# Rotary rotation of key and query tiles handed over 13 steps behind the eviction instead of 7

## The chip, the cores and the metric

The kernel runs on one core of a Trainium2 chip. The metric is the device time of one execution in microseconds (us), smaller is better. The engines are named as in the profile: PE multiplies matrices, PEld is its loading of weights, DVE (VectorE) and ACT (ScalarE) do elementwise work, POOL (GpSimd) does a few small operations, and SP (SyncE) issues the DMAs. Each engine works through its own queue of instructions.

## The reference, cut to what matters

The reference is a trunk of two layers over 256 tokens of width 2048. In each layer one input projection of the normalised `x` feeds two groups of heads: an RWKV-7 scan in both directions, and attention in a window with four key/value heads and sixteen query heads of width 64. Both outputs are gated, joined and sent through one output projection. The part around the change is the rotary position on the attention's keys and queries:

```python
def rope(t, positions):            # half = 32
    ang = positions[:, :, None] * inv
    cos, sin = jnp.cos(ang), jnp.sin(ang)
    t1, t2 = t[..., :half], t[..., half:]
    return concatenate([t1 * cos - t2 * sin, t2 * cos + t1 * sin])
...
    qh = rope(q, positions)
    kh = rope(k_at, positions)
    y_at = window_attention(qh, kh, vh, sink[l])
```

## The kernel before, in words

Everything is kept transposed, 128 channels on the partitions and 256 tokens along the free axis. Products of float32 accuracy are made from parts: a weight tile is split into a high part (ACT, line 221) and a low part (DVE, line 223), the activations likewise, and three matmuls (lines 291 to 293) add up one 128x256 tile. Such three matmuls are one **projection step**; 16 steps make a tile of 128 output channels, and then the tile's eviction function is called.

`Stream` (lines 240 to 273) holds the queue of all projection steps. `run(n)` does n of them. `later(n, fn)` puts `fn` on a timer; the timer is counted down at the end of each step, the one that called `later` included. So `later(7, ...)` calls the function after the sixth step behind the tile's last one, and `later(10, ...)` after the ninth.

The other work of a layer is put between the steps. `window(64, ...)` (line 393) cuts 64 steps into 14 groups of four or five; ahead of each group it advances generators that issue one piece each: `scan_p`, `scan_i` and `scan_b` are three stages of the RWKV scan, `attend` the attention. The order on PE is the order in which the program issues (`manual_schedule`). On the other engines a scheduler chooses the order while the program is built, by its own model of when each instruction will be ready; the chip then runs each engine's list strictly in that order. Instructions issued through `PA` and `PV` (class `InTurn`, line 236) keep the program's order among themselves; in the profile all of them carry line 236 and are told apart by their tiles.

A layer's input tiles come in this order: two low-rank tiles, 32 tiles for the scan in eight windows, the value weights in the first half of a ninth window, the key tiles k0 and k1 in its second half, the query tiles q0 to q3 in a tenth window, and then g0, q4, g1, q5, g2, q6, g3, q7, g4 to g7, gates and queries in turn, in three more. So k0, k1, q0, q1, q2, q3 follow each other every 16 steps, and q4 to q7 come every 32.

The eviction of a key or query tile is `rope_evac` (line 523). It copies the tile from PSUM to `raw` (tile `u`, two buffers, ACT, line 532). Four DMAs on SP's queue (line 534) copy its quarters of 32 partitions, pairwise exchanged, to `rot` (tile `rrot`, one buffer). `turn` (lines 537 to 540) is three DVE instructions: `raw` times the cosines, `rot` times the sines, and their sum in `raw`. `parts` (lines 542 to 544) splits the result into a high part (ACT, into `kr`, or `KA` for keys) and a low part (DVE, into `iu`, `du`, `iuh`, `duh`, or `kd`, `kkr` for keys), which the attention's scores (line 1034) read. `turn` and `parts` are issued by the timers.

The scan's chain on PE that appears below: `scan_i` turns between products in PSUM (`pq`, `pd`, `pf`), which wait for copies by DVE into `tv` (line 907) and by ACT into `QF` and `tt` (lines 900, 868); `scan_b` makes a product `pcc` that waits for ACT's `suv` (line 972). Weight tiles arrive by DMAs on the same SP queue (line 213, `raw<-wi`), into three buffers.

Of the kernel before, what the change touches and what calls it, by code (L numbers as in the profile page):

```python
# [133 lines left out]
def hybrid_trunk_kernel(ctx, tc, xT, wi, wv, wo, par, fing, dup, iup, sink, pos, cst, out):  # L134
# [24 lines left out]
    def st(tag, shape, dt=F32, bufs=1):  # L159
        return sp.tile([128, *shape], dt, tag=tag, name=tag, bufs=bufs)  # L160
# [114 lines left out]
    S = Stream()  # L275
# [145 lines left out]
    def queue_inputs(l):  # L421
# [101 lines left out]
        def rope_evac(place):  # L523
            def evac(pm):
                if not rope:
                    rope.extend((st("TW", [T]), st("XA", [T])))
                    V.tensor_tensor(rope[0], COS, L.norm.rb, op=ALU.mult)
                    V.tensor_tensor(rope[1], SIN, L.norm.rb, op=ALU.mult)
                CR, SR = rope
                raw = st("u", [T], bufs=2)  # L530
                rot = st("rrot", [T])
                A.activation(raw, pm, AF.Copy)
                for q in range(4):
                    SY.dma_start(out=rot[q * 32 : q * 32 + 32, :], in_=raw[(q ^ 1) * 32 : (q ^ 1) * 32 + 32, :])  # L534
                hi, lo = place()

                def turn():
                    PV.tensor_tensor(raw, raw, CR, op=ALU.mult)
                    PV.tensor_tensor(rot, rot, SR, op=ALU.mult)
                    PV.tensor_tensor(raw, raw, rot, op=ALU.add)  # L540

                def parts():
                    PA.activation(hi, raw, AF.Copy)
                    PV.tensor_tensor(lo, raw, hi.bitcast(F32), op=ALU.subtract)

                S.later(7, turn)
                S.later(10, parts)

            return evac

# [692 lines left out]
```

## Time and profile before

| what | value |
|---|---|
| median of 3 runs | 1202.62 us (1201.23 to 1203.34) |
| the profiled execution | 1201.32 us, of which span 1199.5 us |
| mean granted clock of PE | 0.991 |
| rotation DMAs (`rrot<-u`) | 80 of 32.0 KB, 2.1 us to landing (median) |
| `hi` splits on ACT, `lo` splits on DVE | 560 each, 624 and 686 ns (mean) |

The span runs from the first to the last instruction. A timeline row gives the start, the duration, the engine, the line, the operation, its tiles as out<-in, and in brackets the idle time of that engine just before it with what ended it. In rows that merge several DMA issues the duration covers all of them. A row of the waits gives the engine that waited, at which tile, for whom, the total, how often, and the longest.

### The profile page before, as it was taken

The numbers are of one execution on the slowest core, as the hardware profiler recorded it, in microseconds if no ns is written. First come the engines' busy times: TensorE is split into PE (matmuls) and PEld (weight loads), VectorE is DVE, ScalarE is ACT, GpSimd is POOL, SyncE is SP. The second block draws the span as 40 slices with busy tenths as digits, with TensorE's granted clock in tenths as the row PEclk, the third lists the DMA queues.
The fourth block names the chain that finished last, engine by engine and source line by source line (L and its number), as shares of the span: only waits on it lengthen the run. The fifth ranks groups of instructions, "written<-read, shape, count | busy, mean of one in ns | idle before, by whom it ended". The sixth has DMA issues, their size and how long they took to land. (4 is left out here: it accounts for less than half of the span.)

```text
span 1199.5 us, 38085 instructions
## 1 busy us (share of the span) xinstructions
PE 1165.4 (97%) x16151; PEld 1087.2 (91%) x16151; DVE 910.2 (76%) x2019; ACT 776.3 (65%) x1953; POOL 18.9 (2%) x23
## 2 busy tenths in 40 slices
PE   8999999999999999999999999999999999999996
PEld 6998999999888889999999989999998888889996
DVE  6888888888876668866667978887887766786554
ACT  6666776777776557655555766876777665665553
POOL 0000000000000000000000000000000000000000
PEclk8999999999999999999999999999999999999998
DMA  7553333323333434467655443334323333345653
GB/s 254 163 174 124 107 100 114 118 85 115 110 105 106 129 98 137 143 221 249 214 183 166 133 129 113 100 106 127 115 92 99 116 115 131 113 148 186 212 186 121
DMA packets 60410, 166.63 MB, mean 139 GB/s; under 512 B 7728, under 2 KB 22736, under 8 KB 60240
## 3 DMA queue, kind: packets, MB, share of 16 engines
q1 hardware_dynamic: 60240, 164.21, 42.5%
q8 instruction: 126, 2.06, 0.7%
q14 instruction: 44, 0.36, 0.1%
HBM read 157.37 MB, written 4.19 MB: 135 GB/s over the span
## 5 line engine op out<-in xcount | busy, mean ns | idle before, releaser
L291 PE MATMUL pm<-XH,hi 128*128 128x256 f32 x1664 | 495.9, 298 | 3.4 <-ACT XH L183 1.7
L293 PE MATMUL pm<-XH,lo 128*128 128x256 f32 x1664 | 469.9, 282 | 6.2 <-DVE lo L223 6.2
L292 PE MATMUL pm<-XL,hi 128*128 128x256 f32 x1664 | 469.4, 282 | 0.3
L221 ACT ACTIVATE hi<-raw 128x512 fp32r<-128x512 f32 x560 | 327.7, 624 | 194.9 <-PE pm L292 110.3
L223 DVE TENSOR_TENSOR lo<-raw,hi 128x512 fp32r<-128x512 f32 x560 | 369.7, 686 | 97.5 <-ACT hi L221 91.3
L291 PEld LDWEIGHTS pm<-XH,hi 128*128 128x128 f32 x1664 | 315.0, 189 | 18.5 <-ACT XH L183 2.4
L293 PEld LDWEIGHTS pm<-XH,lo 128*128 128x128 f32 x1664 | 315.4, 190 | 8.8 <-DVE lo L223 8.5
L292 PEld LDWEIGHTS pm<-XL,hi 128*128 128x128 f32 x1664 | 315.4, 190 | 1.1 <-DVE XL L184 1.1
L291 PE MATMUL pm<-MH,hi 128*128 128x256 f32 x512 | 144.1, 281 | 0.0
L293 PE MATMUL pm<-MH,lo 128*128 128x256 f32 x512 | 144.0, 281 | 0.0
L292 PE MATMUL pm<-ML,hi 128*128 128x256 f32 x512 | 143.8, 281 | 0.0
L291 PEld LDWEIGHTS pm<-MH,hi 128*128 128x128 f32 x512 | 96.6, 189 | 0.8 <-issue 0.8
L293 PEld LDWEIGHTS pm<-MH,lo 128*128 128x128 f32 x512 | 96.6, 189 | 0.2 <-DVE lo L223 0.2
L292 PEld LDWEIGHTS pm<-ML,hi 128*128 128x128 f32 x512 | 96.6, 189 | 0.0
L907 DVE CAST_PREDICATED tv<-LV,pd 128x256 f16<-128x256 uint8 x80 | 34.4, 430 | 12.8 <-PE pd L906 12.2
L790 DVE TENSOR_TENSOR ge<-pg,C 128x1024 f32<-128x1024 f32 x32 | 38.9, 1221 | 4.4 <-PE pg L784 4.4
L972 ACT ACTIVATE suv<-pcc 64x128 f32<-64x128 f32 x128 | 34.2, 267 | 11.4 <-PE pcc L970 7.1
L900 ACT ACTIVATE QF<-pq 128x256 f16<-128x256 f32 x80 | 30.8, 384 | 14.3 <-PE pq L864 13.8
L1062 ACT ACTIVATE mv<-mv,mx 128x257 f32<-128x257 f32 x64 | 31.8, 501 | 11.3 <-DVE mx L1059 11.3
L956 ACT ACTIVATE rh<-pcc 128x128 f32<-128x128 f32 x64 | 17.5, 273 | 33.2 <-PE pcc L954 32.8
L784 PE MATMUL pg<-mv,bk 64*128 64x128 f32 x512 | 37.2, 285 | 0.3 <-DVE ge L790 0.3
L784 PEld LDWEIGHTS pg<-mv,bk 64*128 64x128 f32 x512 | 31.1, 187 | 2.4 <-DVE ge L790 0.4
(247 smaller groups left out, 1860.1 us busy)
## 6 DMA issues: line engine op xcount, KB each, us to landing
raw<-wi SPq DMA_DIRECT2D x207, 512.0 KB, 3.8
raw<-wo SPq DMA_DIRECT2D x64, 512.0 KB, 4.2
raw<-wv SPq DMA_DIRECT2D x8, 512.0 KB, 3.7
rrot<-u SPq DMA_DIRECT2D x80, 32.0 KB, 2.1
vg<-xT SPq DMA_DIRECT2D x16, 128.0 KB, 4.2
xd<-vg SPq DMA_DIRECT2D x16, 128.0 KB, 3.5
vg<-xd SPq DMA_DIRECT2D x16, 128.0 KB, 3.7
g<-dup SPq DMA_DIRECT2D x16, 97.0 KB
```

What stands on the lines that cost most here:

```text
L221: A.activation(hi[:, q], raw[:, q], AF.Copy)
L223: V.tensor_tensor(lo[:, q], raw[:, q], hi[:, q].bitcast(F32), op=ALU.subtract)
L291: PE.matmul(pm, wh, rh[:, kk, :], start=(kk == 0), stop=False)
L292: PE.matmul(pm, wh, rl[:, kk, :], start=False, stop=False)
L293: PE.matmul(pm, wl, rh[:, kk, :], start=False, stop=(kk == 15))
L784: PE.matmul(pg[:, h, c * 128 : (c + 1) * 128], BK[half[h], d, c, 1 - h : 3 - h, :].rearrange("p s j -> p (s j)"), MV[half[h], d, c].rearra ...
L790: V.tensor_tensor(GEd(d), pg.rearrange("p h (c x) -> p h c x", c=NC), gm[d].unsqueeze(1).unsqueeze(1).to_broadcast([128, 2, NC, 128]), op= ...
L900: A.activation(t_sub(QF), flat4(pq[:, :, 0:128]), AF.Copy)
L907: V.copy_predicated(t_sub(TC), t_mask, flat4(pd[:, :, 0:128]))
L956: A.activation(RH, pc[:, 0], AF.Copy)
L972: A.activation(here(h), pc[half[h], 1], AF.Copy)
L1062: A.activation(Sc[:, h, q, 0:257], Sc[:, h, q, 0:257], AF.Exp, scale=0.125, bias=mx[:, q : q + 1], accum_out=den[:, q : q + 1])
```

## The change

The two timers are longer. `turn` is issued after the twelfth step behind the tile's last one instead of the sixth, `parts` after the fourteenth instead of the ninth. The eviction, the DMAs, the instructions and their buffers are the same.

```diff
-                S.later(7, turn)
-                S.later(10, parts)
+                S.later(13, turn)
+                S.later(15, parts)
```

## The prediction

> **What bounds the kernel now.** I read the page's first part, then the waits of the whole span, then PE's waits in the stretches where key and query tiles are made, and last the timeline there.
>
> ```profile
> PE 1165.4 (97%) x16151; PEld 1087.2 (91%) x16151; DVE 910.2 (76%) x2019; ACT 776.3 (65%) x1953; POOL 18.9 (2%) x23
> ```
>
> PE is busy in 97% of the span; DVE and ACT have room. So a change that adds and removes no instruction can only move PE's idle time, some 34 us by this line, or its clock. DVE's and ACT's waits count where they make PE wait.
>
> ```profile
> DVE u L236 <- DMA rrot<-u: 17.9, 10, 3.2
> ...
> ACT kr L236 <- DVE u L236: 12.7, 10, 3.0
> ```
>
> The rotation is waited for. DVE stands 17.9 us, in 10 waits, at its first instruction until the exchanged copy has landed, and ACT stands 12.7 us at the high part until DVE is done. Each engine takes its queue in order, so all that stands behind these instructions waits too. Now PE, in the stretch from k0 to q3 of layer 0 (352 to 413 us), just behind it (413 to 490), and from k0 to q3 of layer 1 (938 to 998):
>
> ```profile
> PE pf L864 <- DVE tv L907: 1.7, 2, 1.5
> PE pd L906 <- ACT tt L868: 1.0, 1, 1.0
> PE pq L897 <- DVE tv L907: 0.8, 1, 0.8
> ```
>
> ```profile
> PE pcc L977 <- ACT suv L972: 1.8, 1, 1.8
> PE pm L293 <- DVE lo L223: 1.0, 1, 1.0
> ```
>
> ```profile
> PE pf L864 <- DVE tv L907: 1.2, 2, 1.0
> PE pcc L977 <- ACT suv L972: 0.9, 1, 0.9
> PE pd L906 <- ACT tt L868: 0.8, 1, 0.8
> PE pq L897 <- DVE tv L907: 0.8, 1, 0.8
> ```
>
> None of these rows names the rotation, but `tv`, `tt` and `suv` are what stands behind it. The largest, q3 of layer 0, shows it:
>
> ```profile
> 404.58 2.42 SPq L534 DMA_DIRECT2D rrot<-u  x4
> ...
> 409.80 0.42 DVE L236 TENSOR_TENSOR u<-u,TW 128x256 f32<-128x256 f32 x1 [2.31 <-DMA rrot<-u]
> ...
> 410.59 0.28 PE L293 MATMUL pm<-XH,lo 128*128 128x256 f32 x1
> 410.59 0.43 DVE L236 TENSOR_TENSOR u<-u,rrot 128x256 f32<-128x256 f32 x1
> ...
> 411.05 0.42 ACT L236 ACTIVATE kr<-u 128x256 fp32r<-128x256 f32 x1 [2.96 <-DVE u L236]
> ...
> 412.41 0.54 ACT L972 ACTIVATE suv<-pcc 64x128 f32<-64x128 f32 x2
> ...
> 413.01 0.45 PE L977 MATMUL pcc<-suv,bt 128*64 128x64 f32 x8 [1.78 <-ACT suv L972]
> ```
>
> From the first issue to the landing of the last DMA are 409.80 - 404.58 = 5.2 us. DVE idles 2.31 us of it, ACT 2.96 us at `kr`; `suv`, behind `kr` and two weight splits on ACT, starts at 412.41, and PE has idled 1.78 us. That wait has a second price, in the clock (the number after the engines' busy times):
>
> ```profile
> 413.00:418.00 5.00, 4.99 (x47) 4.64 (x49) 3.34 (x9) 2.15 (x5) 0.00 (x0) 0.66 0.34 105
> 998.00:1003.00 5.00, 5.00 (x57) 4.53 (x53) 4.14 (x13) 1.96 (x5) 0.00 (x0) 1.00 0.41 125
> ```
>
> After the wait of 1.78 us PE has a clock of 0.66 for five us, which loses 0.34 x 5 = 1.7 us of work. Behind the same place of layer 1, where the wait was 0.9, it is 1.00.
>
> **The change, part by part.** *The wait for the DMAs goes.* The four DMAs are issued by the eviction and keep their place in SP's queue; only DVE's three and ACT's one and DVE's one instruction behind them move. Is the copy there when the rotation is now handed over, after the twelfth step? For q3 that step is the matmul row at 410.59, which ends at 410.87, 1.07 us after the landing at 409.80. The tightest of the eight tiles with a real wait is k0 of layer 0:
>
> ```profile
> 358.87 0.43 DVE L236 TENSOR_TENSOR u<-u,TW 128x256 f32<-128x256 f32 x1 [1.25 <-DMA rrot<-u]
> ...
> 359.19 0.28 PE L293 MATMUL pm<-XH,lo 128*128 128x256 f32 x1
> ...
> 359.55 0.28 PE L293 MATMUL pm<-XH,lo 128*128 128x256 f32 x1
> ...
> 362.50 0.51 SPq L534 DMA_DIRECT2D rrot<-u  x1
> ```
>
> Its copy has landed by 358.87, and its twelfth step ends at 359.19 + 0.28 = 359.47, 0.6 us later. So I take DVE's waits for `rrot` as gone. The PE waits listed above are then unsupported, but for the one at `pm` (1.0 us), whose cause is the low split of weights: 1.7 + 1.0 + 0.8 + 1.8 = 5.3 us in layer 0 and 1.2 + 0.9 + 0.8 + 0.8 = 3.7 in layer 1, together **9.0 us**. What is late next in each case is PE itself: `tv` and `tt` have only their own product to wait for, and that was done before the group of steps now stalled behind.
>
> *The clock's dip goes* with the 1.78 us wait: **1.7 us**. [...]
>
> *The moved instructions cost their time elsewhere.* The rotation takes 410.59 + 0.43 - 409.80 = 1.22 us of DVE, the high part 0.42 of ACT, the low part about as much of DVE, as before. By the page DVE has 24% of the span idle, so six rotations a stretch find room. New is the shorter way from `turn` to `parts`: two steps instead of three. A step takes 359.55 - 359.19 = 0.36 us, two take 0.72, the rotation 1.22. ACT then waits at least 0.5 us at the high part, on the 12 tiles from k0 to q3: 6.0 us. Behind ACT's high part are queued the weights' high splits, the next eviction and `suv`; PE waits for those. Today 12.7 us of such ACT waits go with 9.0 us on PE, a share of 0.7, so the upper bound is 6.0 x 0.7 = 4.3. The lower bound is zero, by q4, whose rotation found its copy there:
>
> ```profile
> 433.63 0.42 ACT L236 ACTIVATE kr<-u 128x256 fp32r<-128x256 f32 x1 [0.47 <-DVE u L236]
> ```
>
> ACT waits 0.47 us there, and PE's waits from 413 to 490 us hold none that follows from it. That is the nearest row but in an easier stretch, without `scan_i`; I take **2.0 us**, about the middle. A cost below zero is possible as well: with DVE earlier, the 1.0 us at `pm` in 413 to 490 may shrink; I take nothing for it, and keep 1.0 for the low end.
>
> Edits with one answer: the readers of the high and low parts come tens of steps later (k0 and q0 are first read by the scores a window or two later), so five more steps make no one wait; q7 is the closest with 22 steps between its parts and its scores. POOL's queue holds nothing that moves. `PA` and `PV` instructions of the scan issued in the six steps passed now stand ahead of the rotation, where they no longer wait for its DMA.
>
> **Sum.** 9.0 + 1.7 - 2.0 = 8.7 us. The profiled execution took 1201.32 us, and would take 1192.6. The median of the runs, 1202.62, lies 1.3 above it; the same difference from there gives **1193.9**, which I forecast as the median.
>
> **The rivals.** *A, a part of it:* ACT's new wait bites at its upper bound, since DVE starts the rotation late and ACT is only two steps behind, and the clock dips as before. The gain is 9.0 - 4.3 = 4.7, the time 1197.9. For it: every tile from k0 to q3 has splits of weights behind the high part. Against: at the new places the group's urgent copies were issued at the group's start, ahead of the moved instructions.
>
> *B, nothing:* where DVE does the rotation is the scheduler's choice when it thinks the copy has landed, so a later hand-over leaves the order as it is. Time 1202.6. For it: the row of q5 below shows a rotation done long after its hand-over. Against: in the waiting tiles it stands ahead of its copy's landing by up to 2.31 us in the rows above, so the order there is not one that waits for the landing, and a rotation handed over after 359.47 can't be started at 358.87.
>
> *C, slower:* `rrot` has one buffer. The next tile's DMAs can't be issued until the rotation has read it, SP takes its queue in order, and the weight loads queue behind. k1's first such DMA goes out at 362.50, 3.03 us after k0's twelfth step; less the 1.22 us of the rotation, DVE may begin it 1.8 us after the hand-over without harm. How late can DVE be? q5's rotation was handed over at the end of the row at 448.88:
>
> ```profile
> 448.88 0.28 PE L293 MATMUL pm<-XH,lo 128*128 128x256 f32 x1
> ...
> 453.21 0.42 DVE L236 TENSOR_TENSOR u<-u,TW 128x256 f32<-128x256 f32 x1
> ```
>
> It began 453.21 - 449.16 = 4.05 us later. Were that so in all ten close successions (k0 to k1, and on to q3, in two layers), SP would stand 2.2 us in each, 22 us in all. If all of it reached PE the time would be 1202.6 - 10.7 + 22 = 1213.9; the rival decides from the point where more than half of SP's time reaches PE (10.7 of 22). Against it: the rows of k0 and q3 show DVE idle before the rotation, not late, and the late one belongs to the attention's stretch, where successions are 32 steps long. [...]
>
> **How the numbers follow.** The forecast has 0.67, A 0.16, B 0.10, C 0.07. About 0.2%, 2.4 us, is what a measurement of this kernel can tell from no change. The forecast and A are faster by more, less 0.01 for A's tail: 0.82. No change takes B and that tail: 0.11. Slower is C: 0.07. The low end is the full 9.0 + 1.7 and the 1.0 at `pm`, 1202.6 - 11.7 = 1190.9, taken as 1190.5 for the spread of runs. The high end takes in A and stops short of B at 1201.0, which leaves out B and C, 0.17.
>
> **What would show it.** Right: no wait of DVE at `u` for `rrot` in k0 to q3; the PE waits at `pf`, `pd`, `pq` and `pcc` in the two stretches gone or under 0.3 us each; a clock of 1.00 behind q3; ACT's total wait for DVE `u` near 6 us instead of 12.7. Wrong: DVE's queue in the old order with the same waits (B); ACT's waits for `u` at 12 us or more with PE waits at `tt` and `suv` (A); SP waiting at line 534 for DVE `u`, then PE or ACT for `raw<-wi` (C).

## The result, and the profile after

| | before | after |
|---|---|---|
| median | 1201.95 us (1201.23 to 1203.34, 4 runs) | 1190.43 us (1188.86 to 1191.98, 4 runs) |
| the profiled execution | 1201.32 us, span 1199.5 | 1191.98 us, span 1190.2 |

The ratio after to before is 0.9903, 95% interval 0.9886 to 0.992: the change makes the kernel faster by 11.5 us (9.6 to 13.7 by the interval). The forecast was 1193.9 us; the measured time lies 0.07 us below the low end of its range, 1190.5. In a later comparison on another chip the changed kernel took 1189.74 us beside 1200.11, 10.4 us less, ratio 0.991 (0.9892 to 0.9927); one disturbed execution of 2138 us, the profiled one, is left out there, so that its trace says nothing of the waits.

The first part of the page of the changed kernel, and the rotation's two rows among its waits:

```profile
PE 1163.5 (98%) x16151; PEld 1084.7 (91%) x16151; DVE 909.5 (76%) x2019; ACT 776.9 (65%) x1953; POOL 18.6 (2%) x23
```

```profile
DVE u L236 <- DMA rrot<-u: 4.7, 5, 2.1
ACT kr L236 <- DVE u L236: 4.0, 7, 0.8
```

The engines' work is what it was; DVE's wait for the copy fell from 17.9 us to 4.7 and ACT's behind it from 12.7 to 4.0. PE's waits of the changed kernel from k0 to q3 of layer 0 (350 to 411 us), and then behind that (411 to 486):

```profile
PE pn L928 <- ACT tt L868: 0.2, 1, 0.2
```

```profile
PE pm L293 <- DVE lo L223: 1.0, 1, 1.0
```

From k0 to q3 of layer 1 the row at `pn` is the only one, with the same 0.2. All the rows at `pf`, `pd`, `pq` and `pcc` are gone. New is 0.2 us at `pn` in each layer; the 1.0 at `pm` stays. The five us behind q3 of layer 0 in the changed kernel, with the clock behind the five busy times:

```profile
410.00:415.00 5.00, 5.00 (x63) 4.35 (x62) 4.37 (x17) 2.83 (x9) 0.00 (x0) 1.00 0.68 204
```

PE is busy throughout and the clock is 1.00, where it was 0.66 before.

How the gain comes about is seen best at k0 of layer 0. The kernel before, in the timeline, behind the wait of 1.25 us that the prediction shows:

```profile
361.87 0.42 DVE L907 CAST_PREDICATED tv<-LV,pd 128x256 f16<-128x256 uint8 x1
...
362.35 0.30 PE L864 MATMUL pf<-EYE,tv 64*64 64x32 f16 x16 [1.47 <-DVE tv L907]
```

The changed kernel, the same place:

```profile
359.38 1.28 DVE L223 TENSOR_TENSOR lo<-raw,hi 128x512 fp32r<-128x512 f32 x2
360.58 0.42 DVE L907 CAST_PREDICATED tv<-LV,pd 128x256 f16<-128x256 uint8 x1
...
361.05 0.30 PE L864 MATMUL pf<-EYE,tv 64*64 64x32 f16 x16
...
361.24 0.42 DVE L236 TENSOR_TENSOR u<-u,TW 128x256 f32<-128x256 f32 x1
```

DVE's list now has two low splits and `tv` ahead of the rotation. `tv` starts as soon as DVE has done the splits, PE goes on without a gap, and the rotation, now last, finds its copy there. The order of PE's instructions is the same in both kernels.

### The profile page after: what moved, and what is told of

Read it like the earlier page. It is cut to its first block, busy times and chain, and to the rows that moved or that the text cites. A ratio compares the mean times of both kernels' runs of the same rounds, so it can differ in the third digit from the quotient of the medians.

```text
span 1190.2 us, 38093 instructions
## 1 busy us (share of the span) xinstructions
PE 1163.5 (98%) x16151; PEld 1084.7 (91%) x16151; DVE 909.5 (76%) x2019; ACT 776.9 (65%) x1953; POOL 18.6 (2%) x23
## 4 chain that ended last, share of the span: by engine, by line
PE 68%; issue 15%; DVE 11%; ACT 3%; DMA 2%; POOL 1%; SPq 0%; DVEq 0%; POOLq 0%; ACTq 0%
PE pm L291 17%; PE pm L293 14%; PE pm L292 14%; DVE lo L223 3%; PE pg L784 3%; DMA raw<-wi 2%; DVE kd L236 1%; PE pcc L954 1%; PE py L961 1%; PE py L984 1%; PE pcc L977 1%; PE pcc L967 1%; PE pq L897 1%; DVE lw L236 1%; PE pd L906 1%
```

## The experiments

The theory of the prediction: a wait of DVE for the copy at the old place holds up `tv` (on DVE) and, through ACT's high part, `tt` and `suv`; PE pays for those. Its rivals were a new wait of ACT (A), no change of order (B) and SP held by the single `rrot` (C). Two questions came up with the result: whether the size of the term for ACT's shorter way was wrong, and whether the clock's dip really belongs to the wait. All ratios are against the kernel before, timed on the same chip in the same comparison.

**One tile alone, and all but that one.** e1 gives the new timers to q3 alone, e2 to all but q3; each is this edit with the two pairs swapped:

```diff
-        def rope_evac(place):
+        def rope_evac(place, when=(7, 10)):
...
-                S.later(7, turn)
-                S.later(10, parts)
+                S.later(when[0], turn)
+                S.later(when[1], parts)
...
-                inproj(QG0 + 2 * j, rope_evac(q_place(j)))
+                inproj(QG0 + 2 * j, rope_evac(q_place(j), (13, 15) if j == 3 else (7, 10)))
```

> Only q3 is handed over late (13 and 15), the nine other tiles as before (7 and 10). Theory W, that each tile's gain is its own wait for the exchanged copy plus what that wait does to the clock: PE's waits at pcc for suv go (1.8 us in layer 0, 0.9 in layer 1) and the half-speed stretch of 3.4 us behind q3 in layer 0 with them (1.7), 4.4 us together, about 1197.5; the other PE waits at pf, pd and pq stay at 6.3 us. Rival O, that the gain comes from the order of the other instructions as a whole and not from single waits: no such split, anything from 0 to the full 11 us. Rival K, that the clock's dip does not hang on this wait: 2.7 us, about 1199.2, with the dip still in the trace.

> The other half: all tiles late but q3, which stays at 7 and 10. Theory W: PE's waits at pf, pd and pq go (3.5 us in layer 0, 2.8 in layer 1, 6.3 together), those at pcc (1.8 and 0.9) and the dip of the clock stay; about 1195.7. The two halves add up to the whole change. Rival O: no adding up. Rival K: the dip goes here, or stays away by chance, whatever q3's wait is.

e1 took 1196.03 us, ratio 0.9963 (0.995 to 0.9976): 5.0 us below the 1201.01 of the kernel before on that chip. e2 took 1192.66, ratio 0.9933 (0.9918 to 0.9948): 8.35 below. Both gained more than theory W gave them (1197.5 and 1195.7). Together they gain 13.3 us, more than the 11.5 of the whole change; by their intervals, 2.9 to 6.0 and 6.2 to 9.8, the runs cannot tell whether the halves add up exactly. PE's waits of e2 from k0 to q3, layer 0 and then layer 1:

```profile
PE pcc L977 <- ACT suv L972: 1.5, 1, 1.5
```

```profile
PE pcc L977 <- ACT suv L972: 0.7, 1, 0.7
```

The stalls at `pcc` belong to q3 and the others to the other tiles: q3's two waits at `pcc` are all that is left in e2 (beside the 0.2 at `pn`), and they are what is gone in e1. Nothing is handed on to a later tile. The dip behind q3 is gone in e1 together with its wait (clock 1.00 in 410 to 420 us, 0.83 in the kernel before). But the clock does not simply follow a wait: e2, which should have kept the dip, has a wait of 1.5 us at `pcc` and no dip behind it (1.00 in 410 to 420 us), and e1 has a wait of 2.0 us at `pf` in 361 to 364 us, longer than the 1.78 of the kernel before, and no dip there either:

```profile
360.00:370.00 10.00, 7.97 (x160) 7.28 (x161) 7.12 (x15) 4.33 (x10) 0.00 (x0) 1.00 0.42 137
```

**Other delays.** e3 has 9 and 12 steps (two of the six steps by which the change moves the rotation), e4 has 13 and 16 (the old distance of three steps between rotation and high part).

```diff
-                S.later(7, turn)
-                S.later(10, parts)
+                S.later(9, turn)
+                S.later(12, parts)
```

> A smaller delay: the rotation after 8 steps, the parts after 11. Theory W: two steps are 0.7 us where nothing stands between the steps and up to 2 us where scan products do, so DVE's waits for the copy (18 us in all) fall to about half, and half or more of the 9 us on PE goes: 1193 to 1198. Rival O: the time follows the order that comes out and not the delay, so it may lie anywhere, also above the kernel before.

> The changed kernel with the parts one step later (16), so that three steps lie again between rotation and parts. The prediction's term of 2.0 us for the shorter way says that up to 2 us come back: about 1188.5 to 1190.5, with ACT's wait for DVE u shorter by about 0.4 us on each of the 12 close tiles. If that term was zero in truth, as the changed kernel's trace suggests (PE waits of 0.4 us in all), the time is that of the changed kernel within a microsecond, 1190.4.

e3 took 1197.5 us, ratio 0.9973 (0.9963 to 0.9984); e4 took 1189.75, ratio 0.9909 (0.9893 to 0.9926). e4 against 0.9903 and 0.991 of the changed kernel: one more step between rotation and high part buys nothing that can be measured. But it didn't shorten ACT's wait at the high part as expected (4.7 us, against 4.0 in the changed kernel), so e4 alone doesn't price that wait. e3 brings a surprise. Its wait for the copy, over the span:

```profile
DVE u L236 <- DMA rrot<-u: 21.3, 12, 3.5
```

That is more than the 17.9 of the kernel before, where half was expected, and yet e3 is faster. PE's waits at `pf`, `pd`, `pq` and `pcc` are 5.4 us in its two stretches instead of 9.0, and the mean clock of the span is 0.995, 0.991 in the kernel before. What DVE waits in total isn't what PE pays.

**Later still, one buffer and two.** e5 has 15 and 17 steps; e6 the same, with the copies written to `rrot` and to a free tile in turn.

```diff
+        turns = []
...
-                rot = st("rrot", [T])
+                turns.append(pm)
+                rot = st(("rrot", "acc")[len(turns) % 2], [T])
...
-                S.later(7, turn)
-                S.later(10, parts)
+                S.later(15, turn)
+                S.later(17, parts)
```

> Rotation after 14 steps and parts after 16, which puts the parts behind the next tile's eviction; rrot keeps its one buffer. Rival C, that the one buffer holds SP up: SP's waits for DVE u grow from 8.7 us in the changed kernel by about 0.7 us (two steps) in each of ten successions, to 14 us or more, and the weight loads behind them come late, so the time rises by 2 to 7 us over the changed kernel. Theory W, that only the wait for the copy counted: the wait is gone already at 13, nothing more is won, and SP's standing is covered by the weights that are loaded ahead; within 1.5 us of the changed kernel.

> The same delays, but the copies alternate between rrot and another free tile, so that the next tile's DMAs never wait for the rotation. Rival C: what the one buffer cost comes back, 2 to 7 us against the run with one buffer, and SP's waits for DVE u are gone. Theory W: SP's waits are gone as well but the time is that of the run with one buffer within 1.5 us.

> The changed kernel once more, unaltered, beside the three below. It sets the mark for them: 1189 to 1191.5 us. Theory W says that its trace has, as the first one had, no PE wait over 0.3 us between k0 and q3 and no dip of the clock there.

The three ran on one chip. e5 took 1188.65 us, ratio 0.9902 (0.9887 to 0.9917); e6 1188.3, ratio 0.9899 (0.9884 to 0.9914); the changed kernel 1189.74, ratio 0.991 (0.9892 to 0.9927). The intervals overlap, so e6 is the lowest time measured, but not shown to be faster than the change itself. In e5 and e6 DVE no longer waits for the copy at all, ACT's waits at the high part are 0.4 us, and PE has no wait from k0 to q3. So the 4.7 and 4.0 us of such waits in the changed kernel cost it little: the times are 1.1 and 1.4 us apart, within the intervals. SP's waits at the rotation's DMAs, in the changed kernel and then in e5:

```profile
SPq L534 <- ACT hi L221: 52.3, 18, 7.6
SPq L534 <- DVE u L236: 8.7, 8, 1.3
```

```profile
SPq L534 <- ACT hi L221: 35.0, 12, 8.0
SPq L534 <- DVE u L236: 15.2, 10, 3.4
SPq L534 <- ACT kr L236: 7.1, 6, 2.0
```

Rival C's mechanism is there: SP now stands at line 534 until the rotation has read `rrot`, 8.7 us in all, and in e5 15.2. With two buffers the row for `DVE u` is gone and the time is the same within the intervals. SP would have stood at this line anyway: all its waits there add up to 63.1 us in the kernel before, 61.9 in the changed one, 58.2 in e5 and 58.5 in e6. C has a wait but no price.

**A shorter copy.** e7 keeps 7 and 10 steps and lets POOL issue two of the four DMAs.

```diff
-                    SY.dma_start(out=rot[q * 32 : q * 32 + 32, :], in_=raw[(q ^ 1) * 32 : (q ^ 1) * 32 + 32, :])
+                    (SY, G)[q % 2].dma_start(out=rot[q * 32 : q * 32 + 32, :], in_=raw[(q ^ 1) * 32 : (q ^ 1) * 32 + 32, :])
```

> Delays as before the change (7 and 10), but two of the four DMAs of each tile are issued by POOL instead of SP, so that the copy may land earlier: two issues of 0.6 us each less on SP, 1.2 us earlier if POOL is as quick. Theory W, that the wait and not the place in DVE's list made PE wait: DVE's wait for the copy falls from 18 us to about 8, PE's waits between k0 and q3 from 9 us to 3 or 4, the time to 1195 to 1197. Rival O, that the place in the list is what counts: DVE waits less but PE gains under 2 us. If DMAs from POOL land later than those from SP, the wait grows and the time rises; by theory W it then rises by more than half of what DVE waits longer.

It took 1193.7 us, ratio 0.9938 (0.9916 to 0.996). Its wait of DVE, and PE's waits from k0 to q3 of layer 0:

```profile
DVE u L236 <- DMA rrot<-u: 23.7, 11, 4.1
```

```profile
PE pcc L977 <- ACT suv L972: 0.6, 1, 0.6
PE pf L864 <- DVE tv L907: 0.4, 1, 0.4
```

DVE waits longer than in any other run, where theory W expected 8 us; yet PE's stalls fall from 5.3 us to 1.0 in layer 0 and from 3.7 to 2.7 in layer 1, and the mean clock of the span is 0.995. With other DMAs the scheduler made another list on DVE. So this run is no test of the landing alone; it shows again that the sum of DVE's waits decides nothing without what is queued behind each.

**No wait at the old place.** e8 has the old timers and the four DMAs with their places and sizes, but nothing that has to be waited for. It leaves out the exchanged half's product with the sines, so the keys and queries are not rotated.

```diff
-                rot = st("rrot", [T])
+                rot = st("rrot", [T]); cop = st("acc", [T])
...
-                    SY.dma_start(out=rot[q * 32 : q * 32 + 32, :], in_=raw[(q ^ 1) * 32 : (q ^ 1) * 32 + 32, :])
+                    SY.dma_start(out=cop[q * 32 : q * 32 + 32, :], in_=COS[(q ^ 1) * 32 : (q ^ 1) * 32 + 32, :])
...
-                    PV.tensor_tensor(rot, rot, SR, op=ALU.mult)
+                    PV.tensor_tensor(rot, CR, SR, op=ALU.mult)
```

> The old hand-over (7 and 10 steps), but nothing left to wait for: the four DMAs keep their place, size and count, but copy 32 partitions of the cosine table into a free tile, and the rotation's second product takes CR instead of the exchanged copy. Left out: the exchanged half's product with the sines, so the keys and queries are not rotated. Theory P (a wait at DVE's or ACT's queue costs PE by what stands behind it): all waits of DVE at u for rrot are gone, ACT's at kr fall from 12.7 us to about 5, the stalls at pf, pd, pq and pcc fall under 0.3 us each, and the time is 1189 to 1192 us. Rival Q (the place itself costs, since the rotation's 1.2 us of DVE and 0.4 us of ACT stand ahead of the urgent copies at that place whether they wait or not): half or more of the 9 us at pf, pd, pq and pcc stays, and the time is 1195 to 1199 us.

e8 took 1189.92 us, ratio 0.9913 (0.9896 to 0.993), as the changed kernel. From k0 to q3 of layer 0 it has one row:

```profile
PE pf L864 <- DVE tv L907: 0.3, 1, 0.3
```

Layer 1 has the same one row, with 0.3. The scheduler made DVE's list anew here too: the rotation stands at its old place in k1 and q1, and one to three instructions earlier in the other tiles. So its 1.2 us stand ahead of the urgent copies at least as much as before, and PE doesn't pay for them: the wait is the cause, and rival Q is out. One thing more is different in e8: its DMAs don't wait for the eviction either. Moving the rotation behind the landing (the change) and taking away what it waits for (e8) are worth the same.

**A test of the landing that failed.** e9 is the changed kernel with e7's edit.

> The changed kernel (13 and 15 steps) with two of the four DMAs of each tile issued by POOL. DVE's and ACT's order from k0 to q3 is that of the changed kernel; only the landing of the copy differs. Theory P (place decides): DVE's total wait at u for rrot may change from 4.7 us in either direction, up to 10 us, but the stalls at pf, pd, pq and pcc stay under 0.3 us each and the time lies within 1.5 us of the changed kernel, 1188.5 to 1191.5. Rival L (the landing decides): what DVE waits more for the copy, PE waits too in a share of about a half, so with 4 us or more of added waits the stalls are back with 2 us or more and the time is 1192 or over.

It took 1190.48 us, ratio 0.9919 (0.9903 to 0.9935), with the stalls of the changed kernel; but DVE's waits fell to 2.4 us, so nothing was tested. e10 and e11 were made for that, with four copies more, to a free tile, ahead of the four that are needed:

```diff
-                rot = st("rrot", [T])
+                rot, ahead = st("rrot", [T]), st("acc", [T])
...
-                for q in range(4):
-                    SY.dma_start(out=rot[q * 32 : q * 32 + 32, :], in_=raw[(q ^ 1) * 32 : (q ^ 1) * 32 + 32, :])
+                for to, q in [(ahead, q) for q in range(4)] + [(rot, q) for q in range(4)]:
+                    SY.dma_start(out=to[q * 32 : q * 32 + 32, :], in_=raw[(q ^ 1) * 32 : (q ^ 1) * 32 + 32, :])
```

> The changed kernel (13 and 15 steps) with four more copies of the raw tile, into a free tile, issued ahead of the four that are needed: by SP's 0.6 us for each issue the needed copy lands about 2.4 us later. From k0 to q2 DVE's order is that of the changed kernel. Theory P (place decides): DVE's total wait at u for rrot grows from 4.7 us to 12 or more, and the stalls of PE at pf, pd, pq and pcc from k0 to q3 stay at or under 0.5 us each; the time is 1189 to 1192.5 us. Rival L (length decides): PE waits for about half of what DVE waits, as before the change (17.9 us against 9.0), 4 us or more in the two stretches, and the time is 1194 or over.

> The old hand-over (7 and 10 steps) with the same four copies more, so that the needed copy lands about 2.4 us later, and the scheduler, which reckons with them, now puts the rotation behind one to three more instructions on DVE from k0 to q3 (behind the product of the tile's tv in q1 to q3, but not in k0). Theory P: what decides is the place in DVE's list; with the rotation placed later the stalls at pd and pq go, those at pf may stay, and the time is 1190 to 1198 us, faster than the kernel before though the copy lands later. Rival L: a copy that lands 2.4 us later under the old hand-over makes all waits longer, the stalls grow to 15 us or more, and the time is 1205 or over.

e10 took 1200.07 us, ratio 1.0 (0.9988 to 1.0013): the whole gain is gone. The copy came 2.1 to 4.2 us later than in the kernel before (counted from the start of the eviction, at q0, q1 and q3 of both layers). PE's waits from k0 to q3 of layer 0:

```profile
PE pn L928 <- ACT tt L868: 1.7, 1, 1.7
PE py L984 <- ACT suv L972: 1.3, 1, 1.3
PE pg L784 <- DVE ge L790: 0.3, 1, 0.3
```

With layer 1 (1.5 at `py`, 1.3 at `pn`) they are 6.1 us, over the 4 that rival L named, and the wait of 1.7 us is followed by a dip of the clock (0.60 in 408 to 412 us). The stalls at `pf`, `pd`, `pq` and `pcc` did stay away, as theory P said; but its time did not come true, and the place alone doesn't decide: the trace has ACT's list from k0 to q3 and DVE's from q0 to q2 in the order of the changed kernel, and with the longer waits PE stalls at two other products there. The timeline of e10 at q1 of layer 0 shows the way:

```profile
393.56 0.43 DVE L236 TENSOR_TENSOR u<-u,TW 128x256 f32<-128x256 f32 x1 [3.18 <-DMA rrot<-u]
...
395.30 0.42 ACT L236 ACTIVATE kr<-u 128x256 fp32r<-128x256 f32 x1 [2.81 <-DVE u L236]
...
397.02 0.55 ACT L972 ACTIVATE suv<-pcc 64x128 f32<-64x128 f32 x2
...
397.33 0.74 PE L984 MATMUL py<-suv,ge 128*64 128x64 f32 x8 [1.29 <-ACT suv L972]
```

DVE waits 3.18 us, ACT 2.81 at its high part, `suv` is queued behind that, and PE idles 1.29 us. But the length of the wait isn't the price. By the same trace ACT waits 1.99 us at q2 and PE 1.70, while at q0 and q3 ACT waits 2.20 and 2.75 and no wait of PE of 0.15 us or more follows. Each place has a slack, the time until what is queued behind it is needed, and PE pays for what exceeds that. Compare the changed kernel at q3 of layer 0:

```profile
406.77 0.54 ACT L972 ACTIVATE suv<-pcc 64x128 f32<-64x128 f32 x2
406.93 0.42 DVE L236 TENSOR_TENSOR u<-u,TW 128x256 f32<-128x256 f32 x1 [2.07 <-DMA rrot<-u]
...
407.46 0.28 PE L293 MATMUL pm<-XH,lo 128*128 128x256 f32 x1
...
408.03 0.45 PE L977 MATMUL pcc<-suv,bt 128*64 128x64 f32 x8
...
408.18 0.42 ACT L236 ACTIVATE kr<-u 128x256 fp32r<-128x256 f32 x1 [0.43 <-DVE u L236]
```

DVE waits 2.07 us, as long as at q0 of the kernel before (2.04), which cost PE a microsecond; but `suv` now stands ahead of `kr` on ACT, and PE doesn't wait. e11 took 1209.28 us, ratio 1.0081 (1.0064 to 1.0098), against theory P's 1190 to 1198 too. PE's waits of e11 from k0 to q3 of layer 0:

```profile
PE pd L906 <- ACT tt L868: 2.5, 1, 2.5
PE pf L864 <- DVE tv L907: 1.4, 1, 1.4
```

The scheduler did put the rotation later, about as far as the copy: DVE's total wait, 19.4 us, is near the 17.9 of the kernel before, but ACT's at `kr` grew from 12.7 to 21.8. PE's waits from k0 to q3, 5.3 us in layer 0 and 4.3 in layer 1, are under rival L's 15, though its time held; the mean clock of its span is 0.991, against 0.994 in the changed kernel. Both runs also load SP with four more issues for each tile, and ACT's wait for weights of the input projection is 12.4 us in e10 and 12.3 in e11, against 7.8 in the changed kernel and 10.2 in the kernel before; how much of e10's and e11's time is due to that was not separated. So e10 and e11 show that long waits cost at the new place too, and not how many microseconds belong to the rotation alone.

**The kernel before, twice more.** Its profiled execution was taken again, for the clock.

> The kernel before, unaltered, for a second profiled execution. Theory D (the clock's dip follows the wait of 1.78 us behind q3 in layer 0): the wait is there again with 1.6 to 1.9 us, and behind it the clock stands at half for about 3.4 us again, between 411 and 420 us. Rival K (the dip needs this wait and a chance of where it falls in time): the same wait, but no half clock behind it, or one in another place.

> The kernel before, unaltered, for a third profiled execution, as in the run ahead of it. Theory D: half clock for about 3.4 us behind the wait at q3 in layer 0. Rival K: in some executions only, or in another place.

They took 1202.2 and 1200.57 us. PE's waits in layer 0 (352 to 418 us) of the second execution:

```profile
PE pf L864 <- DVE tv L907: 2.1, 2, 1.9
PE pcc L977 <- ACT suv L972: 1.9, 1, 1.9
PE pd L906 <- ACT tt L868: 0.9, 1, 0.9
PE pq L897 <- DVE tv L907: 0.9, 1, 0.9
```

Of the third, the same stretch:

```profile
PE pf L864 <- DVE tv L907: 2.0, 2, 1.8
PE pcc L977 <- ACT suv L972: 1.5, 1, 1.5
PE pd L906 <- ACT tt L868: 1.0, 1, 1.0
PE pq L897 <- DVE tv L907: 1.0, 1, 1.0
PE pcc L954 <- DVE suv L979: 0.3, 1, 0.3
```

In layer 1 (938 to 1003 us) the rows are the same without the last one, and add up to 4.6 us in the second execution and 3.5 in the third.

The clock behind `pf` and behind `pcc` in layer 0, second execution and then third:

```profile
363.00:367.00 4.00, 4.00 (x28) 3.73 (x28) 2.12 (x4) 0.85 (x2) 0.00 (x0) 0.57 0.60 197
414.00:418.00 4.00, 3.63 (x28) 3.52 (x29) 2.00 (x6) 1.17 (x4) 0.00 (x0) 0.57 0.43 128
```

```profile
363.00:367.00 4.00, 4.00 (x70) 3.73 (x59) 2.66 (x5) 0.87 (x2) 0.00 (x0) 0.65 0.72 185
414.00:418.00 4.00, 3.06 (x41) 2.79 (x41) 3.14 (x8) 2.45 (x7) 0.00 (x0) 1.00 0.26 79
```

The stalls are the same in kind in each execution and vary in size. The second execution has two dips, the third one, and that behind `pf`. Theory D in its simple form, a dip behind q3 each time, is out. Rival K is not shown by these three: the longest single waits (1.78 us in the first; 1.87 and 1.9 in the second; 1.8 in the third) had a dip behind them; q3's 1.5 in the third had none (clock 1.00 in 410 to 420 us), nor had the 1.47 at `pf` in the first (1.00 in 360 to 370). That more than the length of the wait decides is shown by other runs, such as e1 with its 2.0 us and no dip.

## Why the prediction was right in its mechanism, and which steps of its sum failed

*The wait goes.* Right for PE: of the 9.0 us listed at `pf`, `pd`, `pq` and `pcc` all are gone, e1 and e2 show that q3's belong to q3 alone, and e8 that they go with the wait. It was too strong for DVE: "So I take DVE's waits for `rrot` as gone" left 4.7 us, 2.07 of it at q3. The working behind it took the twelfth step for the earliest time of a rotation. It isn't: at q3 DVE stands at the rotation from 406.93 - 2.07 = 404.86 us and starts it at 406.93, while the step's last matmul ends at 407.46 + 0.28 = 407.74. A hand-over gives a place in the program from which the scheduler makes its lists; on the chip only the list holds. The same slip weakened the argument against B, which was right in its outcome.

*The shorter way to the high part.* This is the term of the mechanism that failed: 2.0 us were taken, and the changed kernel shows 0.4, the two rows of 0.2 at `pn`. ACT's waits came out at 4.0 us over the span and 3.1 from k0 to q3, about half of the 6.0 reckoned there. Wrong, too, was the share of 0.7 with which they were carried to PE. That share was measured at the old places. At the new ones `suv` stands ahead of the high part at q3; at q1 and q2 `suv` and `tt` still stand behind it, but waits of up to 0.8 us are within the slack there, as against those of e10. e4 buys nothing with one more step, and e5 and e6, with ACT's waits at 0.4, are 1.1 and 1.4 us faster than the changed kernel, with intervals that overlap. The sum with the measured term is 9.0 + 1.7 - 0.4 = 10.3.

*From one execution to the median.* The profiled execution was forecast at 1192.6 and took 1191.98 us, only 0.6 less, though the term above was 1.6 too large. That is luck: PE lost 0.6 us at a late weight tile at the start of layer 1 (649 us) and 0.6 us more than before ahead of 345 us (9.4 us of idle time there before, 10.0 after), which the prediction didn't reckon with. The larger part of the miss is the last step of the sum, "the same difference from there": the median was put 1.3 us above the profiled execution, and it lies 1191.98 - 1190.43 = 1.55 below it. The runs of one kernel differ by 3 us (1188.86 to 1191.98 here), and the difference between one of them and the median did not carry over to another kernel.

Why the medians differ by 11.5 us, and not by 10.3, stays open. The interval, 9.6 to 13.7 us, holds both, and the later comparison gave 10.4. It may be that the execution that was profiled before the change was a mild one. Its stalls and dip made 9.0 + 1.7 = 10.7 us; the second execution has 5.8 + 4.6 and two dips at 1.7, 13.8; the third 5.8 + 3.5 and one dip, 11.0. But their times, 1201.32, 1202.2 and 1200.57 us, don't follow these sums closely, so it is not shown. The low end of the range, 9.0 + 1.7 + 1.0, was built on the first execution alone, with 1.0 at `pm` that didn't move (it is 1.0 after, too), and so fell short by 0.07 us.

*The clock.* The 1.7 us were right for the profiled execution, but the dip doesn't follow q3's wait each time. In the first trace the clock is 0.50 from 413.73 to 417.14 us, 3.41 us long, and 1.00 from there to 1188.56; in the changed kernel it is 1.00 from 15.15 to 1179.09 us. Behind five single waits of PE a dip lost 1.7 us: behind the 1.78 us of the first execution, the 1.87 and 1.9 of the second and the 1.8 of the third (0.83 over ten us each time), and behind the 1.70 of e10 (0.98 over 403 to 408 us and 0.60 over 408 to 412). Behind e1's 2.0 us it was 1.00 (360 to 370 us), and e7, which has a wait of 1.9 us at `pf` in layer 1, has a mean clock of 0.995 over the span. So the length of a wait doesn't decide alone. Where a wait falls may count too: the changes of the clock in the first trace (4.13, 7.55, 14.37, 413.73, 417.14 and 1188.56 us) lie 1, 2, 117, 1 and 226 times 3.413 us apart, those in the trace of the changed kernel (4.91, 11.74, 15.15 and 1179.09) 2, 1 and 341 times. That the place decides was not shown.

*The rivals.* A lost by its time (1190.43 against 1197.9), but its mechanism is real: with the copy later, in e10, ACT's high part holds `suv` and PE pays. B was out, since DVE's list changed at k0. C's wait of SP came, 8.7 us, with no price. Of the signs named, the clock of 1.00 behind q3 and the waits of PE under 0.3 us came true; DVE without a wait at q3 did not; ACT's total was 4.0 instead of "near 6".

What stays open: the size of the slack at each place, how much of e10's loss is SP's load, why the medians differ by more than the sum, and what beside the length of a wait of PE decides over a dip of the clock.

## What to carry to other kernels

When an instruction that waits for a DMA stands in an in-order queue, look at what is queued behind it and when that is needed, not at the length of the wait: 21.3 us of waiting cost less here than 17.9 had. Hand such work over late enough that its data is there, and test the margin by making the transfer later, since the whole gain was gone here with four more DMAs a tile and a copy that came 2 to 4 us later. And sum stalls over several profiled executions before setting the end of a range: here the same kernel lost 10.7, 13.8 and 11.0 us; and don't carry the difference between one execution and the median from one kernel to another.

## What the runs showed of the hardware

Five single waits of PE of 1.7 to 1.9 us came with a dip of the clock, at 1.7 us each: one in the first execution of the kernel before, two in the second, one in the third and one in e10. In the first, the clock was 0.50 for 3.41 us. A wait of 2.0 us in e1 left the clock at 1.00, and e7 with one of 1.9 us had a mean clock of 0.995, which stays unexplained. In the traces of the kernel before and of the changed one the clock changed only at times that lie whole multiples of 3.413 us apart within a trace: 1, 2, 117, 1 and 226 in the one, 2, 1 and 341 in the other.
